# A macaron transformer trunk: cast order in the first turn, and two 512-column products behind the last transposes of x

## The chip, the cores and the metric

The kernel runs on one core of a Trainium2 chip. The metric is the device time of one launch in microseconds (us). The engines are TensorE (PE, with PEld for its weight loads), VectorE (DVE), ScalarE (ACT), GpSimd (POOL) and SyncE (SP). Each executes its own instructions in order and waits for the others through semaphores.

## The reference, cut to what matters

A sequence of 512 rows of width 1024 in float32 passes through two layers. Each has two half-step SwiGLU FFNs, one at either end, with a token mixer (differential attention in layer 0, a pooling mixer in layer 1) and a cross attention into 256 memory rows between them.

```python
D_MODEL, SEQ, DEPTH, D_FF = 1024, 512, 2, 2816

def swiglu_ffn(x, w_in, w_out):
    h = x @ w_in
    g, u = jnp.split(h, 2, axis=-1)
    return (jax.nn.silu(g) * u) @ w_out

for i in range(DEPTH):
    x = layer_norm(a * x + 0.5 * swiglu_ffn(x, ffn_w_in[i, 0], ffn_w_out[i, 0]), ...)
    ...
    x = layer_norm(a * x + h, ...)
    x = layer_norm(a * x + memory_cross_attention(x, mem, ...), ...)
    x = layer_norm(a * x + 0.5 * swiglu_ffn(x, ffn_w_in[i, 1], ffn_w_out[i, 1]), ...)
```

## The kernel before

**Pairs.** A float32 value is kept as a high part in float32r and a low part that holds the rest. A product of two such pairs is three products on PE (`mm3`, L210 to L212): high by high, the high weight by the low x (`xl`), and the low weight (`wl`) by the high x. A weight tile arrives raw by DMA. `operand` then makes its pair: a cast on ACT for the high part (`wh`, L689) and a subtraction on DVE for the low one (`wl`, L691).

**An FFN block.** There are four, starting at about 0, 750, 1080 and 1600 us; "block 1" is the first. `ffn` goes through the eleven units of 256 columns of w_in in turns of three and then two, each turn together with the w_out products of units that are finished (`down`, 512 columns wide, tiles `px`, `py`, `pz`). The first turn has units alone, in three lanes.

**A unit.** `up` computes gate and value of a unit by seven products instead of eight (Strassen-Winograd): x is cut into four parts, and products 0 to 6 are taken with those parts and with sums of them, in the order 0 (into PSUM tile x), 1 (y), 3 (z), 6 (z, added), 4 and 5 (x), 2. Each has 24 matmuls of 256 columns: two halves of 128 weight columns, four k steps, three products. The sums of x, called s1 to s4, are made on DVE by `second_factors` (L656, L661) and cut into pairs by `part` (`xe`, L125 on ACT and L126 on DVE): part 6 is s4, 4 is s2, 5 is s3. The weights of product 3 come out of those of product 0 by a DMA that adds to them in SBUF (`more`, L683, on POOL's queue, in tiles `ra`), as do the later ones; a raw tile's next add waits until its low part has been taken. Products 1 and 6 read tiles `rc`, loaded on SP's queue (L679). There are four buffers of `wh` and `wl`, four of `ra` and three of `rc`.

**Lanes.** The generators of three units are advanced in turn by `ffn`: a `yield` in `up` ends a lane's step, and the program order that results, with the scheduler's own rules and `issue_after` (an order that it must keep), sets the order on each engine. Block 1 starts while x and the weights still arrive (`at_start`). There the products of lanes 0 and 2 are taken by passes in places (`by_passes`, L716): all products on the high weights first, then those on the low ones. In this block the cast of lane 2's third operand, tile `ra`, precedes that of lane 0's `rc` for product 6.

**Blocks 2, 3 and 4** begin with the end of a layer norm: PE transposes the last rows of x (L494, eight of 128 x 128 into `pt`), between the products of the first lane, and goes on with the unit's second product, y.

Of the kernel before, what the change touches and what calls it, by code (L numbers as in the profile page):

```python
# [109 lines left out]
class Trunk:  # L110
# [407 lines left out]
    def ffn(self, layer, j, ln, beside=()):  # L518
# [58 lines left out]
        for turn in range(n):  # L577
            behind = turn == n - 1
            for step in range(1 if turn == 0 else 0, 9 if behind else 7):
                if turn == 0 and step in (2, 3):  # L580
                    next(second)
                if step == 4:
                    if behind:
                        coming = [self.plain_down(w_out, layer, j, ln, beside)]
                    else:
                        coming = start(turn + 1)
                        if at_start and turn == 0:
                            with self.tc.issue_after(self.last_load.ins):
                                next(downs[1])
                if behind and step in (4, 6, 7, 8):  # L590
                    next(coming[0])
                if behind and step > 3:
                    few(beside, 2)

                for lane, w in enumerate(works[: None if not behind or step > 1 else -1]):
                    if not (at_start and turn == 0 and lane < 2 and step == 1):
                        next(w, None)
                if turn == 1 and step == 3:
                    self.seven_of[self.waiting[0]] = self.seven(self.waiting[1])
            works = coming  # L600
# [14 lines left out]
    def second_factors(self):  # L615
# [15 lines left out]
        def part(i, x, o=slice(0, H)):  # L631
            return self.split(F[i][0][:, :, o], F[i][1][:, :, o], x)
# [21 lines left out]
        nc.vector.scalar_tensor_tensor(s2, s1, -1.0, a11, ALU.mult, ALU.subtract)  # L654
        s4 = s1
        nc.vector.scalar_tensor_tensor(s4, s2, -1.0, a12, ALU.mult, ALU.subtract)  # L656
        part(6, s4)
        yield
        part(4, s2)
        s3 = a21  # L660
# [4 lines left out]
    def up(self, w, u, lane, early, between):  # L665
# [16 lines left out]
        def more(t, *block):  # L682
            nc.gpsimd.dma_start(t, source(*block), accum_op=ALU.add)  # L683

        def operand(raw, behind=None):
            v = self.hl([P, 4, H])
            act, dve = behind or (None, None)
            with self.tc.issue_after(act.ins) if behind else nullcontext():
                hi = nc.scalar.copy(v[0], raw)  # L689
            with self.tc.issue_after(dve.ins) if behind else nullcontext():  # L690
                lo = nc.vector.tensor_sub(v[1], raw, v[0].bitcast(F32))  # L691
            splits.append((hi, lo))
            return v
# [28 lines left out]
        splits = []  # L722

        third = lane == 2
        at_start = early and self.begins is None
        sp = lambda: self.tmp("ha" if third else "sp", (P, 2, H))
        yz = "py" if third else "yz"
        ra = load("ra", 1, 1)
# [1 line left out]
            between()  # L730
        rc = load("rc", 2, 1)
        yield
        v = operand(ra, self.turned_parts if third and at_start else None)
        if early and lane == 0:
            self.first_split = splits[0]
        more(ra, 1, 2)
# [3 lines left out]
        if at_start and lane == 0:  # L740
            by_passes(x, v, 0, (0,))
            yield
        v2 = early > 1 and operand(rc, self.turned if at_start else None)
        if v2:
            self.second_split = splits[-1]
            yield
# [5 lines left out]
        nc.scalar.copy(p1, x)  # L752
        yield
        y = bank(self.aux("y", yz))
        v2 = v2 or operand(rc, self.made_parts if third and at_start else None)
        with self.behind() if at_start else nullcontext():
            product(y, v2, 1, True, lane != 1 and at_start)
        hr = self.tmp("hr", (P, 2, S))
        h1, h2 = hr[:, :, :H], hr[:, :, H:]
        nc.vector.tensor_tensor(h1, y, p1, ALU.add)  # L760
        nc.scalar.activation(h1, h1, AF.Silu)
        yield
        v = operand(ra, self.made_parts if at_start and lane == 0 else None)
        if at_start and lane == 0:
            self.made_parts = splits[-1]
            yield
        z = bank(self.aux("z", yz))
        product(z, v, 3, True)
        more(ra, 2, 2)
        rd = load("rc", 2, 2)  # L770
        p5 = sp()
        nc.scalar.copy(p5, z)
        yield
        product(z, operand(rd), 6)
        more(rd, 1, 2)
        yield
        product(x, operand(ra), 4)
# [911 lines left out]
```

## Time and profile before

| | us |
|---|---|
| median of three runs | 1927.93 (1924.76 to 1930.44) |
| profiled execution | 1927.77 |
| its span | 1926.0 |
| PE busy | 1900.1 |
| DVE busy | 1564.4 |
| ACT busy | 1022.8 |
| POOL busy | 320.6 |

The page's times are of one profiled execution. PE's instructions overlap: a matmul starts before the one ahead of it has ended, so the distance from start to start, and not the length of one, tells how fast PE goes. A row of the timeline gives the start, the length, engine, line, operation and tiles, and in brackets how long the engine stood idle before it and which engine ended that. The granted clock is the share of full speed that the chip allowed PE.

### The profile page before, as it was taken

Reading aid. Unit: us, or ns where it says so; the run is one execution under the profiler, and the core shown is the slowest. Engines: PE = TensorE matmul, PEld = TensorE weight load, DVE = VectorE, ACT = ScalarE, POOL = GpSimd, SP = SyncE. Lnnn points to the kernel's source line nnn. Section 1 sums busy time; section 2 is a strip of 40 time slices with the busy share of each in tenths; the row PEclk is TensorE's granted clock in tenths of the full one; section 3 lists DMA queues with packets and bytes.
Section 4 is the critical chain, followed back from the end, with each engine's and each line's share of the span. In section 5 each row is a group of like instructions: output and inputs, shape, how many; then the busy total and the mean of one; then the engine's idle time right before and its main releaser. Section 6 shows DMA issues by size and latency. Waiting matters only on the chain.

```text
span 1926.0 us, 32482 instructions
## 1 busy us (share of the span) xinstructions
PE 1900.1 (99%) x13066; PEld 1741.3 (90%) x13066; DVE 1564.4 (81%) x2264; ACT 1022.8 (53%) x1580; POOL 320.6 (17%) x278
## 2 busy tenths in 40 slices
PE   9999999999999999999999999999999999999998
PEld 8999998888878888999998999999899889999997
DVE  7888989888967558888888988888887568998886
ACT  6555554567755435655554655455455436555553
POOL 2112121111210002211210321112130012111210
PEclk9999999999999999999999999999999999999999
DMA  9978772322124317978686588788344437877861
GB/s 236 220 170 184 167 141 86 91 66 88 55 99 153 110 66 192 181 175 164 139 192 179 105 179 171 176 164 186 111 132 132 132 88 157 182 160 170 184 133 56
DMA packets 246742, 277.94 MB, mean 144 GB/s; under 512 B 8256, under 2 KB 212544, under 8 KB 246592
## 3 DMA queue, kind: packets, MB, share of 16 engines
q0 software_dynamic: 92928, 92.29, 31.3%
q1 hardware_dynamic: 153664, 183.59, 29.7%
q8 instruction: 102, 1.67, 0.4%
q14 instruction: 48, 0.39, 0.1%
HBM read 273.75 MB, written 2.10 MB: 143 GB/s over the span
## 4 chain that ended last, share of the span: by engine, by line
PE 77%; DVE 14%; ACT 4%; issue 2%; DMA 2%; POOL 1%; SPq 0%; DVEq 0%; ACTq 0%; POOLq 0%
PE x L210 7%; PE x L211 7%; PE x L212 7%; PE z L212 4%; PE z L210 4%; PE z L211 4%; PE ps L210 3%; PE ps L212 3%; PE ps L211 3%; PE px L210 2%; PE px L212 2%; PE px L211 2%; PE y L212 2%; DVE wl L691 2%; PE xq L210 1%
## 5 line engine op out<-in xcount | busy, mean ns | idle before, releaser
L683 POOL DMA_DIRECT2D ra<-in_ffn_w_in_dram x132 | 171.3, 1318 | 988.9 <-DVE wl L691 812.2
L689 ACT CAST wh<-ra 128x1024 fp32r<-128x1024 f32 x176 | 185.0, 1053 | 215.6 <-PE x L211 66.6
L691 DVE TENSOR_TENSOR wl<-ra,wh 128x1024 fp32r<-128x1024 f32 x176 | 214.2, 1220 | 71.2 <-ACT wh L689 70.9
L689 ACT CAST wh<-rc 128x1024 fp32r<-128x1024 f32 x132 | 138.9, 1053 | 107.6 <-PE x L211 41.8
L210 PE MATMUL x<-xe,wh 128*128 128x256 f32 x704 | 195.2, 277 | 0.0
L211 PE MATMUL x<-xe,wh 128*128 128x256 f32 x704 | 195.1, 277 | 0.0
L212 PE MATMUL x<-xe,wl 128*128 128x256 f32 x704 | 195.0, 277 | 0.0
L125 ACT CAST wh<-b 128x1024 fp32r<-128x1024 f32 x112 | 117.8, 1052 | 132.3 <-PE x L211 65.6
L691 DVE TENSOR_TENSOR wl<-rc,wh 128x1024 fp32r<-128x1024 f32 x132 | 159.7, 1219 | 27.1 <-ACT wh L689 26.1
L126 DVE TENSOR_TENSOR wl<-b,wh 128x1024 fp32r<-128x1024 f32 x112 | 136.7, 1221 | 40.8 <-ACT wh L125 40.8
L210 PE MATMUL x<-xh,wh 128*128 128x256 f32 x536 | 148.9, 278 | 0.0
L211 PE MATMUL x<-xl,wh 128*128 128x256 f32 x536 | 148.5, 277 | 0.0
L212 PE MATMUL x<-xh,wl 128*128 128x256 f32 x536 | 148.5, 277 | 0.0
L211 PEld LDWEIGHTS x<-xe,wh 128*128 128x128 f32 x704 | 132.7, 189 | 1.4
L210 PEld LDWEIGHTS x<-xe,wh 128*128 128x128 f32 x704 | 132.2, 188 | 1.3
L212 PEld LDWEIGHTS x<-xe,wl 128*128 128x128 f32 x704 | 132.2, 188 | 0.0
L126 DVE TENSOR_TENSOR wl<-raw,wh 128x1024 fp32r<-128x1024 f32 x64 | 83.0, 1301 | 42.4 <-ACT wh L125 41.6
L211 PEld LDWEIGHTS x<-xl,wh 128*128 128x128 f32 x536 | 101.0, 189 | 0.7
L210 PEld LDWEIGHTS x<-xh,wh 128*128 128x128 f32 x536 | 100.6, 188 | 0.7
L212 PEld LDWEIGHTS x<-xh,wl 128*128 128x128 f32 x536 | 100.6, 188 | 0.0
L212 PE MATMUL z<-xe,wl 128*128 128x256 f32 x352 | 98.4, 280 | 2.2 <-DVE wl L691 2.2
L211 PE MATMUL z<-xe,wh 128*128 128x256 f32 x352 | 98.3, 279 | 0.4 <-DVE xe L126 0.4
(442 smaller groups left out, 6304.0 us busy)
## 6 DMA issues: line engine op xcount, KB each, us to landing
ra<-in_ffn_w_in_dram POOLq DMA_DIRECT2D x132, 512.0 KB, 7.0
rc<-in_ffn_w_in_dram SPq DMA_DIRECT2D x88, 512.0 KB, 5.7
b<-in_ffn_w_out_dram SPq DMA_DIRECT2D x76, 512.0 KB, 4.8
ra<-in_ffn_w_in_dram SPq DMA_DIRECT2D x44, 512.0 KB, 4.8
rc<-in_ffn_w_in_dram POOLq DMA_DIRECT2D x44, 512.0 KB, 7.9
raw<-in_xa_wkv_dram SPq DMA_DIRECT2D x16, 1024.0 KB, 5.4
raw<-in_da_w_qkv_dram SPq DMA_DIRECT2D x16, 512.0 KB, 5.3
raw<-in_xa_wq_dram SPq DMA_DIRECT2D x8, 1024.0 KB, 5.1
```

Source lines behind the costliest of these rows:

```text
L125: self.nc.scalar.copy(hi, src),
L126: self.nc.vector.tensor_sub(lo, src, hi.bitcast(F32)),
L210: mm(out, w[0], x[0], start=start, stop=False, skip_group_check=again)
L211: mm(out, w[0], x[1], start=False, stop=False, skip_group_check=again)
L212: self.last_mm = mm(out, w[1], x[0], start=False, stop=stop, skip_group_check=again)
L683: nc.gpsimd.dma_start(t, source(*block), accum_op=ALU.add)
L689: hi = nc.scalar.copy(v[0], raw)
L691: lo = nc.vector.tensor_sub(v[1], raw, v[0].bitcast(F32))
```

## The change

In block 1's first turn, lane 0 makes the pair of its `rc` tile for product 6 in a step of its own, one step earlier, and lane 2's third operand is ordered behind it (`made_parts`) and behind the pair of s4 (`factor_parts`). Lane 2's product 3 is taken by passes. In blocks 2, 3 and 4 the first lane issues two products of 512 columns into y's bank, weights against weights, ahead of product 1; product 1 starts with `start=True` and overwrites them.

```diff
@@ -595,6 +595,8 @@
                 for lane, w in enumerate(works[: None if not behind or step > 1 else -1]):
                     if not (at_start and turn == 0 and lane < 2 and step == 1):
                         next(w, None)
+                    if at_start and turn == 0 and lane == 1 and step == 2:
+                        next(works[0])
                 if turn == 1 and step == 3:
                     self.seven_of[self.waiting[0]] = self.seven(self.waiting[1])
             works = coming
@@ -654,7 +656,7 @@
         nc.vector.scalar_tensor_tensor(s2, s1, -1.0, a11, ALU.mult, ALU.subtract)
         s4 = s1
         nc.vector.scalar_tensor_tensor(s4, s2, -1.0, a12, ALU.mult, ALU.subtract)
-        part(6, s4)
+        self.factor_parts = part(6, s4)
         yield
         part(4, s2)
         s3 = a21
@@ -682,12 +684,11 @@
         def more(t, *block):
             nc.gpsimd.dma_start(t, source(*block), accum_op=ALU.add)
 
-        def operand(raw, behind=None):
+        def operand(raw, *behind):
             v = self.hl([P, 4, H])
-            act, dve = behind or (None, None)
-            with self.tc.issue_after(act.ins) if behind else nullcontext():
+            with self.after([act for act, _ in behind]):
                 hi = nc.scalar.copy(v[0], raw)
-            with self.tc.issue_after(dve.ins) if behind else nullcontext():
+            with self.after([dve for _, dve in behind]):
                 lo = nc.vector.tensor_sub(v[1], raw, v[0].bitcast(F32))
             splits.append((hi, lo))
             return v
@@ -722,7 +723,7 @@
         splits = []
 
         third = lane == 2
-        at_start = early and self.begins is None
+        at_start = early > 0 and self.begins is None
         sp = lambda: self.tmp("ha" if third else "sp", (P, 2, H))
         yz = "py" if third else "yz"
         ra = load("ra", 1, 1)
@@ -730,7 +731,7 @@
             between()
         rc = load("rc", 2, 1)
         yield
-        v = operand(ra, self.turned_parts if third and at_start else None)
+        v = operand(ra, *((self.turned_parts,) if third and at_start else ()))
         if early and lane == 0:
             self.first_split = splits[0]
         more(ra, 1, 2)
@@ -740,7 +741,7 @@
         if at_start and lane == 0:
             by_passes(x, v, 0, (0,))
             yield
-        v2 = early > 1 and operand(rc, self.turned if at_start else None)
+        v2 = early > 1 and operand(rc, *((self.turned,) if at_start else ()))
         if v2:
             self.second_split = splits[-1]
             yield
@@ -752,26 +753,40 @@
         nc.scalar.copy(p1, x)
         yield
         y = bank(self.aux("y", yz))
-        v2 = v2 or operand(rc, self.made_parts if third and at_start else None)
+        v2 = v2 or operand(rc, *((self.made_parts,) if third and at_start else ()))
         with self.behind() if at_start else nullcontext():
+            if early > 1 and not at_start:
+                wide = v2[0][:, :2].rearrange("p k n -> p (k n)")
+                for _ in range(2):
+                    nc.tensor.matmul(
+                        y.rearrange("p j n -> p (j n)"), v2[0][:, 0, :P], wide, start=True, stop=True
+                    )
             product(y, v2, 1, True, lane != 1 and at_start)
         hr = self.tmp("hr", (P, 2, S))
         h1, h2 = hr[:, :, :H], hr[:, :, H:]
         nc.vector.tensor_tensor(h1, y, p1, ALU.add)
         nc.scalar.activation(h1, h1, AF.Silu)
         yield
-        v = operand(ra, self.made_parts if at_start and lane == 0 else None)
-        if at_start and lane == 0:
+        if not at_start or lane == 1:
+            v = operand(ra)
+        elif third:
+            v = operand(ra, self.made_parts, self.factor_parts)
+        else:
+            v = operand(ra, self.made_parts)
             self.made_parts = splits[-1]
             yield
         z = bank(self.aux("z", yz))
-        product(z, v, 3, True)
+        product(z, v, 3, True, third and at_start)
         more(ra, 2, 2)
         rd = load("rc", 2, 2)
         p5 = sp()
         nc.scalar.copy(p5, z)
         yield
-        product(z, operand(rd), 6)
+        v = operand(rd)
+        if at_start and lane == 0:
+            self.made_parts = splits[-1]
+            yield
+        product(z, v, 6)
         more(rd, 1, 2)
         yield
         product(x, operand(ra), 4)
```

ACT in block 1's first turn. The tiles: `ra` and `rc` are raw weights, `hr` the gate on its way through silu, `hb` and `sr` hold the sums s4, s2, s3 of x, `sp` and `ha` keep copies of the PSUM tiles x and z. Before:

```order
L752 COPY ha<-x 128x512
L689 CAST wh<-ra 128x1024
L689 CAST wh<-rc 128x1024
L761 ACTIVATE hr<-hr 128x2x256
L689 CAST wh<-rc 128x1024
L125 CAST xe<-hb 128x1024
L772 COPY sp<-z 128x512
L125 CAST xe<-sr 128x1024
L772 COPY sp<-z 128x512
L125 CAST xe<-hb 128x1024
L689 CAST wh<-rc 128x1024
L689 CAST wh<-ra 128x1024
```

Now (a line that was L689 is L690, L761 is L768, L772 is L783):

```order
L753 COPY ha<-x 128x512
L690 CAST wh<-rc 128x1024
L768 ACTIVATE hr<-hr 128x2x256
L783 COPY sp<-z 128x512
L125 CAST xe<-hb 128x1024
L690 CAST wh<-ra 128x1024
L125 CAST xe<-sr 128x1024
L783 COPY sp<-z 128x512
L690 CAST wh<-rc 128x1024
L125 CAST xe<-hb 128x1024
L690 CAST wh<-rc 128x1024
L783 COPY ha<-z 128x512
```

The first cast of `ra` stands four places further down, behind that of `rc`, a silu, a copy of z and the cast of `xe` from s4.

DVE at the same place, before:

```order
L760 TENSOR_TENSOR hr<-y,ha 128x2x256
L656 SCALAR_TENSOR_TENSOR hb<-sr,hb 128x1024
L691 TENSOR_TENSOR wl<-ra,wh 128x1024
L661 TENSOR_TENSOR hb<-hb 128x1024
L126 TENSOR_TENSOR xe<-hb,xe 128x1024
L126 TENSOR_TENSOR xe<-sr,xe 128x1024
L691 TENSOR_TENSOR wl<-rc,wh 128x1024
L126 TENSOR_TENSOR xe<-hb,xe 128x1024
L691 TENSOR_TENSOR wl<-rc,wh 128x1024 x2
L691 TENSOR_TENSOR wl<-ra,wh 128x1024 x3
```

Now (L691 is L692, L656 is L658, L661 is L663):

```order
L767 TENSOR_TENSOR hr<-y,ha 128x2x256
L658 SCALAR_TENSOR_TENSOR hb<-sr,hb 128x1024
L692 TENSOR_TENSOR wl<-rc,wh 128x1024
L663 TENSOR_TENSOR hb<-hb 128x1024
L126 TENSOR_TENSOR xe<-hb,xe 128x1024
L692 TENSOR_TENSOR wl<-ra,wh 128x1024
L126 TENSOR_TENSOR xe<-sr,xe 128x1024
L692 TENSOR_TENSOR wl<-rc,wh 128x1024
L126 TENSOR_TENSOR xe<-hb,xe 128x1024
L692 TENSOR_TENSOR wl<-rc,wh 128x1024
L692 TENSOR_TENSOR wl<-ra,wh 128x1024 x3
```

The first subtraction for `rc` moves up to where that for `ra` stood, and that for `ra` stands behind the first `xe`.

PE at the start of block 2, at the end of the transposes (X_77 is the last tile of x), before:

```order
L211 MATMUL x<-xl,wh 128x256
L212 MATMUL x<-xh,wl 128x256
L494 MATMUL pt<-ident,X_77 128x128 x8
L210 MATMUL y<-xh,wh 128x256
L211 MATMUL y<-xl,wh 128x256
L212 MATMUL y<-xh,wl 128x256
```

Now:

```order
L211 MATMUL x<-xl,wh 128x256
L212 MATMUL x<-xh,wl 128x256
L494 MATMUL pt<-ident,X_77 128x128 x8
L761 MATMUL y<-wh 128x512 x2
L210 MATMUL y<-xh,wh 128x256
L211 MATMUL y<-xl,wh 128x256
L212 MATMUL y<-xh,wl 128x256
```

Two products of 512 columns stand between the transposes and y. Blocks 3 and 4 have the same two rows at the same place. In blocks 2 and 3 the scheduler also moves some casts of `ra` and `rc` on ACT and their subtractions on DVE ahead of those for `xe`; on POOL one add to an `rc` tile moves ahead of one to an `ra` tile in block 1; SP's order stays.

## The prediction

> **What bounds the kernel now.** I read the page first: the busy times, then the chain that ended last.
>
> ```profile
> span 1926.0 us, 32482 instructions
> PE 1900.1 (99%) x13066; PEld 1741.3 (90%) x13066; DVE 1564.4 (81%) x2264; ACT 1022.8 (53%) x1580; POOL 320.6 (17%) x278
> PE 77%; DVE 14%; ACT 4%; issue 2%; DMA 2%; POOL 1%; SPq 0%; DVEq 0%; ACTq 0%; POOLq 0%
> ```
>
> PE is busy for 1900.1 of 1926.0 us, so there are two ways to gain: fill its few gaps, or make its products follow each other faster. So I looked at windows of 10 us, where PE's count matters more than its busy share.
>
> ```profile
> 30.00:40.00 10.00, 8.48 (x70) 7.87 (x68) 7.06 (x8) 7.22 (x10) 2.56 (x2) 1.00 1.20 216
> 40.00:50.00 10.00, 8.93 (x64) 8.93 (x65) 7.57 (x7) 4.53 (x6) 6.47 (x5) 0.83 0.88 126
> 60.00:70.00 10.00, 10.00 (x91) 10.00 (x90) 9.01 (x11) 4.81 (x7) 0.00 (x0) 1.00 1.10 337
> 780.00:790.00 10.00, 10.00 (x87) 10.00 (x87) 5.93 (x5) 3.46 (x4) 5.99 (x5) 1.00 1.18 179
> 1610.00:1620.00 10.00, 9.27 (x77) 8.68 (x76) 10.00 (x11) 7.49 (x10) 3.88 (x3) 1.00 0.50 98
> ```
>
> The columns are the window, its length, busy us and count of PE, PEld, DVE, ACT and POOL, the granted clock, the DMA share and GB/s. Two things stand out. In the first block's first turn (30 to 50 us) PE has gaps, and the granted clock falls to 0.83. And at 780 us, in block 2, a PE that is just as full at clock 1.00 starts 87 products in 10 us where block 1 starts 91.
>
> **The gap in block 1.** PE's timeline there:
>
> ```profile
> 34.85 0.28 PE L211 MATMUL z<-xl,wh 128*128 128x256 f32 x1
> 35.15 0.38 PE L212 MATMUL z<-xh,wl 128*128 128x256 f32 x1
> 37.75 0.36 PE L210 MATMUL z<-xe,wh 128*128 128x256 f32 x1
> 38.51 0.38 PE L211 MATMUL z<-xe,wh 128*128 128x256 f32 x1 [0.40 <-DVE xe L126]
> 41.07 0.53 PE L212 MATMUL z<-xe,wl 128*128 128x256 f32 x1 [2.17 <-DVE wl L691]
> 44.39 0.36 PE L212 MATMUL z<-xe,wl 128*128 128x256 f32 x1
> 50.72 0.28 PE L210 MATMUL x<-xe,wh 128*128 128x256 f32 x1
> 44.94:80.64 35.70, 35.70 (x317) 35.70 (x316) 26.49 (x34) 19.18 (x25) 7.91 (x7) 1.00 1.16 259
> ```
>
> The last row, a window, gives the full pace: some 315 products in 35.70 us, 0.1133 us from start to start. The three lanes' product 6 (3 x 24 = 72 products) takes 50.72 - 37.75 = 12.97 us instead of 72 x 0.1133 = 8.16: 4.81 us lost. Some 3.2 us of it is two waits, for product 6's left operand (`xe`, DVE) and for the low part of lane 0's weights (`wl`). The rest follows from them: from 41.07 to 44.39 there are 15 steps from product to product, 0.22 us each, nearly double, and the granted clock of that window is 0.83. A small wait at 35.15 adds about 0.3 (0.30 instead of 0.11 to its start, and 0.1 behind it). Together 5.1 us.
>
> Why `xe` and `wl` are late stands on ACT and DVE, and in two transfers:
>
> ```profile
> 27.80 0.57 ACT L752 COPY ha<-x 128x512 f32<-128x512 f32 x1
> 32.78 1.05 ACT L689 CAST wh<-ra 128x1024 fp32r<-128x1024 f32 x1 [4.41 <-DMA ra<-in_ffn_w_in_dram]
> 33.74 1.05 ACT L689 CAST wh<-rc 128x1024 fp32r<-128x1024 f32 x1
> 36.16 1.04 ACT L125 CAST xe<-hb 128x1024 fp32r<-128x1024 f32 x1
> 30.31 0.69 DVE L760 TENSOR_TENSOR hr<-y,ha 128x512 f32<-128x512 f32 x1
> 30.91 1.22 DVE L656 SCALAR_TENSOR_TENSOR hb<-sr,hb 128x1024 f32<-128x1024 f32 x1
> 33.87 1.23 DVE L691 TENSOR_TENSOR wl<-ra,wh 128x1024 fp32r<-128x1024 f32 x1 [1.74 <-ACT wh L689]
> 39.80 1.22 DVE L691 TENSOR_TENSOR wl<-rc,wh 128x1024 fp32r<-128x1024 f32 x1
> 13.90 5.50 SPq L679 DMA_DIRECT2D rc<-in_ffn_w_in_dram  x2
> rc<-in_ffn_w_in_dram SPq DMA_DIRECT2D x1, 512.0 KB, 13.1
> ```
>
> ACT executes in order and stands 4.41 us at the cast of lane 2's third operand (call it ra2'), whose data an accumulating DMA brings at 32.7. Behind it wait the cast of lane 0's `rc` (rd0), a silu, and the cast of `xe`. Yet rd0 had been issued at 13.90 and took 13.1 us (the last row, for that issue), so it was there at 27.0.
>
> **What the change makes of it.** It puts rd0's cast ahead of ra2', and the silu, the copy of z and the cast of `xe` as well. Working through with the durations above (on ACT one starts about 0.95 after the one before, on DVE 1.14):
> - ACT: rd0 at 28.3, within the former wait; the silu at 31.05, since DVE's `hr` ends at 31.0; the copy of z at about 32.1, when lane 1 takes over from lane 0 on PE; `xe` at 32.6 (s4, the DVE row at 30.91, ends at 32.13); ra2' at 33.5 to 34.6.
> - PE asks for ra2' where it does now, one product ahead of 34.85, at 34.74: no wait, or at most 0.25 us if a step of ACT slips.
> - DVE: rd0's low part at 32.05, the next sum at 33.2, `xe`'s low part at 34.3 to 35.5, ra2's low part at 35.45 to 36.7. PE now takes lane 2's z in passes: 16 products on the high part, then one of product 6, then 8 on the low part, which begins at 34.74 + 17 x 0.113 = 36.7: just in time again.
> - Then product 6 has both operands from 37.6 on; the low parts of lanes 1 and 2 (37.75 and 40.05 on DVE) are done 1 to 2 us ahead of PE.
>
> So PE runs through and product 6 ends at about 45.7 instead of 50.72: **-5.0 us**. From both sides: 5.1 if nothing is late, and 4.6 if both "just in time" places each slip a quarter of a microsecond. No operation is added in block 1. What lies behind must come 5 us earlier too: weights. The tightest of the later casts waits for a DMA even now:
>
> ```profile
> 71.38 1.05 ACT L689 CAST wh<-ra 128x1024 fp32r<-128x1024 f32 x1 [3.15 <-DMA ra<-in_ffn_w_in_dram]
> 72.46 1.23 DVE L691 TENSOR_TENSOR wl<-ra,wh 128x1024 fp32r<-128x1024 f32 x1 [2.50 <-ACT wh L689]
> 77.92 0.28 PE L210 MATMUL x<-xh,wh 128*128 128x256 f32 x1
> ```
>
> Its low part is done at 73.7, and its product starts at 77.92 and needs the low part two products later, at 78.15. Of these 4.4 us of cover nothing is left if that transfer stays where it is: 0.6 us lost, and 1 to 2 us if a second cast is late in the same way. But it should move too, because buffers come free earlier and the DMA engines have room in 40 to 50 us (share 0.88), so I take nothing off.
>
> The rule that I weigh here is in the Trainium skill, "TensorE: Matmul & The Clock Gate", section "What's actually happening": the array drops to half rate after an idle window of some 3.4 us and needs about as long of work to come back. The trace agrees: 3.2 us of waits, then 3.3 us at nearly doubled pitch. By it a rest of wait of half a microsecond costs only itself.
>
> **The two products in blocks 2, 3 and 4.** Here PE doesn't wait; it is in a slower rhythm. The same 256-column product comes in two paces:
>
> ```profile
> 761.80:818.22 56.42, 56.42 (x482) 56.42 (x480) 48.36 (x57) 35.13 (x46) 14.19 (x11) 1.00 0.88 169
> 1088.60:1145.01 56.41, 56.41 (x481) 56.41 (x480) 48.13 (x57) 33.94 (x45) 14.22 (x11) 1.00 0.92 180
> 1616.82:1659.80 42.98, 42.98 (x381) 42.98 (x381) 35.73 (x44) 24.70 (x32) 12.95 (x10) 1.00 1.10 209
> 821.02:826.48 5.46, 5.46 (x50) 5.46 (x48) 5.46 (x6) 2.74 (x3) 1.27 (x1) 1.00 0.45 128
> 1078.44:1081.37 2.93, 2.93 (x26) 2.92 (x25) 2.93 (x5) 0.84 (x1) 2.60 (x2) 1.00 1.05 158
> 760.81 1.03 PE L494 MATMUL pt<-ident,X 128*128 128x128 f32 x8
> 761.60 0.36 PE L210 MATMUL y<-xh,wh 128*128 128x256 f32 x1
> 818.22 0.40 PE L210 MATMUL px<-wh,ha 128*128 128x512 f32 x1
> 743.41 1.04 PE L494 MATMUL pt<-ident,X 128*128 128x128 f32 x8
> 744.20 0.48 PE L210 MATMUL ps<-q,oT 128*128 128x512 f32 x1
> 744.75 0.40 PE L212 MATMUL ps<-q,oT 128*128 128x512 f32 x1
> ```
>
> A window's count takes in a product or two at its ends. In blocks 2 and 3 some 479 products follow the transposes at 56.42 / 479 = 0.1178 us, without a wait; block 4, which has waits in its z, comes out of them at 42.98 / 380 = 0.1131. A pace, once taken, holds until something of another width or a wait comes. Behind 512-column products the 256-column ones are fast: the row 821.02:826.48 is 48 of them (0.1138), and so are all such places of the turns that follow. The exception is the row 1078.44: 24 products in 2.93 less the transposes' start, at 0.1178, behind 18 products of 512. So a product of 512 columns gives the fast pace mostly, not always.
>
> Cost: the rows from 743.41 show transposes followed by 512 columns: the first starts 0.79 behind the transposes, as y does now (760.81, 761.60), and the third product starts 744.75 - 744.20 = 0.55 later. So y's first product comes 0.55 later, while its second follows at 0.12 instead of 0.20 (761.60 and the window's start at 761.80): **+0.47 us** net for a block. Gain, if y falls into the fast pace: 480 x (0.1178 - 0.1133) = 2.15 us, so **-1.68 us** for block 2 and the same for block 3. The ends are +0.47 and -1.68 a block; I take the fast one, by the many 512-column runs that end so.
>
> The scheduler also moves casts forward in blocks 2 and 3 (ra and rc ahead of `xe`). They land more than 2 us before PE asks, also at the fast pace, so they count for nothing; DVE is 5.93 busy of 10 in 780 to 790, which leaves room to catch up. In block 4 the 0.47 us go into waits that are there today: PE stands at 9.27 in 1610 to 1620 while DVE is busy for 10.00 of 10.00, and DVE's chain, not PE's start, sets when PE goes on. So **0**; without that cover +0.47, and +1.7 if the waits now end in the slow pace (380 x 0.0045).
>
> A page speaks against this part: the Trainium skill, "TensorE: Matmul & The Clock Gate", section "Wait — 56ns, not 53.3ns?", gives a warm product of N columns one fixed distance, N / 2.4 GHz plus 2.5 ns, an estimate of 109 ns for 256 and 216 for 512. By that there is no second pace, and six more products only cost 6 x 0.216 = 1.3 us. The windows above measure 113 and 118 for the same shape, so the measurement decides that two paces exist; whether two products switch them, no row shows.
>
> **The sum.** Against the profiled execution's 1927.77 us (1926.0 of span and 1.8 around it; the median of the runs is 1927.93): -5.0 - 2 x 1.68 + 0 = -8.4, so **1919.5 us**.
>
> **Rivals.**
> 1. *The pace stays slow behind the two products.* For it: the row at 1078.44, and that the slow pace also follows the transposes directly. Against it: the row at 821.02. Then 1927.8 - 5.0 + 2 x 0.47 = 1923.7 us. The page's rule above gives nearly the same time.
> 2. *Part of block 1's gain is lost*: a transfer sets the later casts (1 to 2 us, above), or the "just in time" place at 34.6 leaves a small wait behind which the slow pace holds, some 400 products x 0.0045 = 1.8 us; or block 4 falls into the slow pace (+1.7). With fast blocks 2 and 3: about 1921.4. Against it: PE's gaps at 35.15 and 38.51 both ended in the fast pace.
> 3. *Slower: the slow pace holds beyond the first turn.* The turns behind it alternate 48 products of 256 columns with 12 of 512, 8.2 us together. At 0.1178 the 48 take 5.65 instead of 5.46; 12 of 512 in the slow pace take 821.02 - 818.22 = 2.80 where the fast take 8.2 - 5.46 = 2.74: +0.25 for a pair, and some 26 pairs from 821 to 1035 make +6.5 us a block. With blocks 2 and 3 so: 1927.8 - 5.0 + 0.9 + 13 = 1936.7. It decides from 16 pairs on. Against it: today the slow first turn runs into 818.22 and comes out fast at 821.02.
> 4. *The cast order doesn't come about on the chip as in the program* (ra2' needed earlier than I work out, and PE's wait only moves): block 1 then gains 0 to 2, and with fast blocks 2 and 3 the total is 1922.4 to 1924.4. For it: two places are just in time. Against it: the wait of 4.41 us, with rd0's data there.
>
> **How the numbers follow.** Forecast 0.54; rival 1 0.20; rival 2 0.10; rival 3 0.10; rival 4 0.06. A measurement here tells no change from a change of 0.3%, or 5.8 us: faster is below 1922.1. That holds for the forecast and half of rival 2: 0.59. Same: rivals 1 and 4 and the rest of 2: 0.31. Slower: rival 3, 0.10. Range: from 1916.5, where block 1 gives 5.1, block 4 turns out fast too and the turn behind starts a bit earlier, to 1925.5, which takes in rivals 1 and 2 and part of 4.
>
> **What would show it.** Right: in 30 to 50 us PE starts some 88 in each 10 us at clock 1.00, ACT has no wait of 4 us, and x's first product behind product 6 starts near 45.7; in 780 to 790 PE starts 91, and px of block 2 starts about 1.7 us earlier relative to y's transposes. Wrong: ACT still waits at `wh<-ra` with `xe` behind it; 87 in 780 to 790; or under 48 products in 5.5 us behind 821.

## The result, and the profile after

The changed kernel takes **1921.58 us** (median of seven runs, 1920.15 to 1922.73) against 1927.43 for the kernel before (seven runs). The ratio is 0.9972, with a 95% interval of 0.9961 to 0.9982: 5.9 us or 0.3% less, just at the bound of what a measurement tells from no change, where the prediction said 1919.5 and 8.4 us. The profiled execution took 1921.52 us, its span 1919.7, so 6.3 us less than the profiled execution of before (1926.0 of span). This is the windows view of the changed kernel (window, length, busy us and count of PE, PEld, DVE, ACT and POOL, granted clock, DMA share, GB/s):

```profile
30.00:40.00 10.00, 10.00 (x88) 9.94 (x88) 10.00 (x10) 8.13 (x11) 4.27 (x4) 1.00 1.20 218
40.00:50.00 10.00, 10.00 (x88) 10.00 (x86) 6.27 (x6) 4.47 (x5) 6.04 (x5) 1.00 1.24 199
60.00:70.00 10.00, 10.00 (x87) 10.00 (x86) 6.60 (x8) 4.49 (x5) 1.28 (x1) 1.00 1.07 371
780.00:790.00 10.00, 10.00 (x91) 10.00 (x90) 5.53 (x6) 4.26 (x5) 3.37 (x3) 1.00 1.22 192
1100.00:1110.00 10.00, 10.00 (x91) 10.00 (x90) 6.79 (x6) 5.30 (x6) 6.75 (x6) 1.00 1.05 162
```

The gap in block 1 is gone: 88 products in each of the first two windows, where 70 and 64 stood, and the clock is 1.00. At 780 and 1100 us PE starts 91 instead of 87; for 1100, this was the row of the kernel before:

```profile
1100.00:1110.00 10.00, 10.00 (x87) 10.00 (x86) 9.36 (x9) 6.88 (x9) 6.09 (x5) 1.00 1.07 156
```

But the row 60:70, which had 91, now has 87: block 1 has taken on the slow pace that blocks 2 and 3 lost. The starts of the same instructions in the two PE timelines show where the time went:

| start of | before | changed | difference | gained since the row above |
|---|---|---|---|---|
| first px, block 1 | 80.64 | 77.56 | -3.08 | -3.08 |
| last transposes of x, block 2 | 760.81 | 758.04 | -2.77 | +0.31 |
| first px, block 2 | 818.22 | 813.78 | -4.44 | -1.67 |
| last transposes of x, block 3 | 1087.60 | 1083.11 | -4.49 | -0.05 |
| first px, block 3 | 1145.01 | 1138.85 | -6.16 | -1.67 |
| last transposes of x, block 4 | 1602.84 | 1596.38 | -6.46 | -0.30 |
| first px, block 4 | 1659.78 | 1653.38 | -6.40 | +0.06 |

Three of the four terms came out as predicted in this pair of profiles: -1.67 for blocks 2 and 3 each (-1.68 was said) and +0.06 for block 4 (0). Block 1 gave 3.08 instead of 5.0. Its timeline, ACT's row first, then DVE's, then PE's:

```profile
33.94 1.04 ACT L690 CAST wh<-ra 128x1024 fp32r<-128x1024 f32 x1
34.65 1.22 DVE L126 TENSOR_TENSOR xe<-hb,xe 128x1024 fp32r<-128x1024 f32 x1
35.79 1.22 DVE L692 TENSOR_TENSOR wl<-ra,wh 128x1024 fp32r<-128x1024 f32 x1
35.04 0.38 PE L717 MATMUL z<-xh,wh 128*128 128x256 f32 x1
37.07 1.19 PE L717 MATMUL z<-xh,wl 128*128 128x256 f32 x8
77.56 0.40 PE L210 MATMUL px<-wh,ha 128*128 128x512 f32 x1
38.10:77.56 39.46, 39.46 (x338) 39.46 (x336) 31.21 (x40) 22.38 (x29) 9.51 (x8) 1.00 1.15 254
```

Lane 2's third operand, once the cause of a wait of 4.41 us, is cast at 33.94 and wanted at 35.04. Its low part is ready at 35.79 + 1.22 = 37.01, and the low pass begins at 37.07. That is the "just in time" place: the pass of eight takes 1.19 us where seven steps of 0.113 and one length of 0.28 make 1.07. The 0.1 us is nothing. What follows is not: from 38.10 to px 335 products take 39.46 us, 0.1178 each.

Behind the transposes of block 2:

```profile
758.04 1.03 PE L494 MATMUL pt<-ident,X 128*128 128x128 f32 x8
758.83 0.71 PE L761 MATMUL y<-wh 128*128 128x512 f32 x2
759.38 0.28 PE L210 MATMUL y<-xh,wh 128*128 128x256 f32 x1
813.78 0.39 PE L210 MATMUL px<-wh,ha 128*128 128x512 f32 x1
759.38:813.78 54.40, 54.40 (x482) 54.40 (x480) 47.29 (x57) 34.85 (x45) 14.17 (x11) 1.00 0.92 175
1084.45:1138.85 54.40, 54.40 (x481) 54.40 (x480) 47.34 (x57) 33.52 (x44) 14.19 (x11) 1.00 0.94 184
```

The two products take 0.55 us (759.38 - 758.83), as worked out, and the 480 behind them take 54.40 us, 0.1133 each, where the kernel before needed 56.42 for 479.

### The profile page after: what moved, and what is told of

Its sections match the earlier page's. It is cut to its first block, busy times and chain, and to the rows that moved or that the text cites. A ratio compares the mean times of both kernels' runs of the same rounds, so it can differ in the third digit from the quotient of the medians.

```text
span 1919.7 us, 32489 instructions
## 1 busy us (share of the span) xinstructions
PE 1895.9 (99%) x13072; PEld 1738.2 (91%) x13072; DVE 1563.6 (81%) x2264; ACT 1023.4 (53%) x1580; POOL 319.8 (17%) x278
## 4 chain that ended last, share of the span: by engine, by line
PE 78%; DVE 13%; ACT 4%; DMA 2%; issue 2%; POOL 1%; SPq 0%; DVEq 0%; ACTq 0%; POOLq 0%
PE x L210 7%; PE x L211 7%; PE x L212 7%; PE z L212 4%; PE z L210 4%; PE z L211 4%; PE ps L210 4%; PE ps L212 4%; PE ps L211 4%; PE px L210 2%; PE px L212 2%; PE px L211 2%; PE y L212 2%; PE xq L210 1%; PE xq L211 1%
## 5 line engine op out<-in xcount | busy, mean ns | idle before, releaser
L690 ACT CAST wh<-ra 128x1024 fp32r<-128x1024 f32 x176 | 185.1, 1054 | 207.5 <-PE x L211 66.5
L692 DVE TENSOR_TENSOR wl<-ra,wh 128x1024 fp32r<-128x1024 f32 x176 | 213.9, 1220 | 67.1 <-ACT wh L690 66.4
L690 ACT CAST wh<-rc 128x1024 fp32r<-128x1024 f32 x132 | 138.9, 1053 | 104.9 <-PE x L211 40.4
L125 ACT CAST wh<-b 128x1024 fp32r<-128x1024 f32 x112 | 117.8, 1052 | 128.9 <-PE x L211 65.1
L692 DVE TENSOR_TENSOR wl<-rc,wh 128x1024 fp32r<-128x1024 f32 x132 | 159.8, 1218 | 26.8 <-ACT wh L690 26.8
L125 ACT CAST wh<-raw 128x1024 fp32r<-128x1024 f32 x64 | 66.5, 1049 | 59.3 <-PE xq L211 21.0
```

The lines of the kernel that those rows point to most:

```text
L125: self.nc.scalar.copy(hi, src),
```

## The experiments

In what follows the "distance" of a block is that from the start of the last single transpose (0.03 us ahead of what follows it) to the first px: 56.65 us in blocks 2 and 3 before, 54.98 in the changed kernel. Each profile is one execution; the times are medians, and each ratio is to runs of the kernel before on the same chip.

**1. The first turn alone.**

```diff
-            if early > 1 and not at_start:
...
-                for _ in range(2):
-                    nc.tensor.matmul(..., v2[0][:, 0, :P], wide, start=True, stop=True)
```

> The changed kernel without its six products of 512 columns: only the first turn's order. Theory A (the two products set the pace of blocks 2 and 3, the cast order sets block 1, and nothing else matters): block 1's first px starts at 77.6 as in the changed kernel, 3.1 us earlier than before; in blocks 2 and 3 the distance from the last transposes to px is 57.4 us again, at 87 products in 10 us; time 1927.4 - 3.0 = 1924.4. Theory B (blocks 2 and 3 got faster because everything ahead of them moved, so that the pace fell otherwise): the distance stays near 55.8 and the time near 1921.5.

Measured: 1922.34 us, ratio 0.9976 (0.9965 to 0.9987). The profiled execution (1920.18, the fastest of its seven runs) was faster than A allowed, and its windows and rows say why:

```profile
38.10:75.72 37.62, 37.62 (x335) 37.62 (x333) 29.58 (x36) 20.86 (x27) 9.18 (x8) 1.00 1.17 261
756.49:810.78 54.29, 54.29 (x482) 54.29 (x480) 47.04 (x57) 35.03 (x46) 14.22 (x11) 1.00 0.92 175
1081.14:1137.56 56.42, 56.42 (x482) 56.42 (x481) 48.16 (x57) 33.95 (x45) 14.22 (x11) 1.00 0.92 181
```

Block 1 ends in the fast pace here (px at 75.72, 4.9 us earlier than in the first profile of before), with the same cast order. Block 2 is fast without any 512-column product (54.29 for some 480), and block 3 slow (56.42). So neither A nor B as put: against that profile the cast order does give the full 4.9 us where the pace stays fast, and block 2's pace isn't the same in every execution. What differs in block 2 lies ahead of the transposes: the first product's run x is slow there (0.1178), where it was fast (0.1133) in the profile of before.

**2. The six products alone**, on the kernel before.

```diff
         with self.behind() if at_start else nullcontext():
+            if early > 1 and not at_start:
...
+                for _ in range(2):
+                    nc.tensor.matmul(..., v2[0][:, 0, :P], wide, start=True, stop=True)
             product(y, v2, 1, True, lane != 1 and at_start)
```

> The kernel before with the six products of 512 columns alone. Theory A: px of block 1 at 80.6 as before, blocks 2 and 3 55.8 us from the last transposes to px, 1.66 less each, block 4 unchanged within 0.2; time 1927.4 - 3.3 = 1924.1. Theory B: blocks 2 and 3 at 57.4 or more, +0.47 each, time 1928.4.

Measured: 1925.84 us, ratio 0.9991 (0.9983 to 1.0), less than A said, and its interval reaches no change at all; the profiled execution (1926.58) was the slowest of the eleven.

```profile
762.72:817.17 54.45, 54.45 (x481) 54.42 (x480) 47.39 (x57) 34.85 (x45) 14.16 (x11) 1.00 0.91 175
1087.82:1142.25 54.43, 54.43 (x481) 54.40 (x480) 47.38 (x57) 33.56 (x44) 14.19 (x11) 1.00 0.95 185
1612.20:1658.46 46.26, 46.26 (x396) 46.26 (x394) 37.75 (x46) 26.20 (x34) 13.38 (x11) 1.00 1.03 194
1610.72 0.38 PE L212 MATMUL z<-xh,wl 128*128 128x256 f32 x1 [0.87 <-DVE wl L691]
```

Blocks 2 and 3 are fast, as A has it. Only block 3 tells for the products, though: x of block 2 is slow here, and in number 1 y came out fast behind a slow x without them. Block 4 was slow behind its wait for DVE: some 393 products in 46.26 us, 0.1177 each, and its distance grew from 56.17 to 57.87. That took back 1.7 us in this execution. The casts' 0.24% and the products' 0.09% add up to the change's 0.28% within their intervals.

A misses in block 1: px starts at 79.15 and not at 80.6, with the old cast order and the same wait of 2.17 us for `wl` ahead of 41.02. The clock tells why. In all fourteen traces the granted clock switches only at whole multiples of 3.413 us from the first switch. These are such stretches around the wait, the first two in the profile of before, the last two here:

```profile
37.74:41.15 3.41, 0.83 (x5) 0.44 (x3) 3.21 (x4) 3.41 (x5) 0.00 (x0) 1.00 1.04 159
41.15:44.57 3.42, 3.42 (x16) 3.42 (x17) 3.42 (x4) 1.27 (x2) 2.04 (x2) 0.50 0.33 33
35.94:39.35 3.41, 2.66 (x22) 2.27 (x20) 2.21 (x3) 3.41 (x6) 0.67 (x1) 1.00 1.23 194
39.35:42.77 3.42, 1.75 (x15) 1.75 (x16) 3.42 (x4) 3.02 (x4) 1.28 (x1) 1.00 0.57 91
```

Before, the wait filled one stretch nearly whole (PE busy for 0.83 us), and the next one ran at 0.50. Here it is split between two stretches (2.66 and 1.75 us busy), and the clock stays at 1.00. Number 8 has the dip again, behind a stretch with 1.58 us. The mean clock of a whole run shows it too: 0.998 in both profiles with the dip, 0.999 here. Of the 66 timed runs of the kernel before beside the experiments, 36 have 0.998 or less, and their medians are 0.6 to 1.6 us above those of the other 30 on each of the four occasions; of number 2's eleven, five have 0.998. All runs with the new cast order have 0.999.

**3. No wait at the low pass.** DVE's sum s3 behind lane 2's low part:

```diff
+            self.third_parts = splits[-1]
...
-        nc.vector.tensor_tensor(s3, a11, a21, ALU.subtract)
+        with nullcontext() if self.begins else self.tc.issue_after(self.third_parts[1].ins):
+            nc.vector.tensor_tensor(s3, a11, a21, ALU.subtract)
```

> The changed kernel, with DVE's sum s3 ordered behind the low part of lane 2's third operand, which is then ready some 0.8 us before PE asks for it. Theory A (the 0.09 us that PE waits for this low part at 37.28 puts all that follows into the slow pace, 342 products at 0.1178): the wait is gone, the products from 35 us to px stay at 0.1133, px starts at 77.6 - 1.6 = 76.0, time 1921.6 - 1.6 = 1920.0. Theory C (the slow pace there has another cause, such as the denser load of casts and transfers): 87 or 88 products in 10 us remain, px at 77.4 to 77.6, time 1921.5.

Measured: 1920.48 us, ratio 0.9965 (0.9952 to 0.9977). In this execution weights arrived about 1 us later at the start of the block, so that px starts at 77.24; the pace is what answers.

```profile
36.49 1.22 DVE L693 TENSOR_TENSOR wl<-ra,wh 128x1024 fp32r<-128x1024 f32 x1
38.26 1.07 PE L718 MATMUL z<-xh,wl 128*128 128x256 f32 x8
38.50:77.24 38.74, 38.74 (x344) 38.74 (x343) 30.92 (x37) 21.76 (x29) 9.82 (x8) 1.00 1.17 259
```

The low part is ready at 37.71, half a microsecond ahead of the pass; the pass takes 1.07 us, and some 342 products behind it take 38.74 us, 0.1133 each. C is out: the same casts and transfers with the same density run at the fast pace when the wait is gone. That the wait is what decides isn't shown by this one execution, since number 9 stays fast with it.

**4. Two 512-column products in block 1**, behind lane 2's z.

```diff
+        if third and at_start:
+            idle = self.aux("idle", "py")
...
+                for _ in range(2):
+                    self.last_mm = nc.tensor.matmul(idle, v[0][:, 0, :P], wide, start=True, stop=True)
```

> The changed kernel with two more products of 512 columns in block 1, into a bank that nobody reads, right behind the low pass of lane 2's z (38.1 us). Theory A (a 512-column product ahead of a run of 256 ones puts it into the fast pace, wherever it stands): the slow pace from 37.28 lasts for 8 products only, the 334 behind it go at 0.1133; -334 x 0.0045 + 0.46 = -1.0 us, px at 76.5, time 1920.5. Theory C: the pace behind them stays 0.1178, px at 78.0, time 1922.0.

Measured: 1920.23 us, ratio 0.9965 (0.9952 to 0.9979), its five runs within 0.8 us. Behind the products the run to px is fast, as A has it:

```profile
38.93:76.91 37.98, 37.98 (x337) 37.98 (x335) 29.83 (x36) 21.08 (x27) 9.06 (x8) 1.00 1.17 260
```

But the wait at the low pass had left the fast pace already in this execution, so the row doesn't show that the products turned it.

**5. One product instead of two** in blocks 2 to 4 (`range(1)` for `range(2)`).

> The changed kernel with one 512-column product instead of two behind the last transposes of x. The scheduler then leaves the casts of blocks 2 and 3 in their old order. Theory A (the pace is set by the last distance from start to start ahead of the run; 203 or 204 ns behind the transposes is followed by the slow pace, 205 and more by the fast one): one product leaves a distance of some 315 ns, so y is fast in blocks 2 and 3, 0.23 us shorter than with two: 54.75 us from the last transpose to px, time 1921.3. Theory D (it takes two, because only 230 to 236 ns between 512-column products is followed by the fast pace; or the new cast order of blocks 2 and 3 is what helps): y is slow, 56.65 + 0.3, time 1925.

Measured: 1920.79 us, ratio 0.997 (0.9958 to 0.9982), and block 2 in the profile:

```profile
757.81 0.48 PE L761 MATMUL y<-wh 128*128 128x512 f32 x1
758.12 0.28 PE L210 MATMUL y<-xh,wh 128*128 128x256 f32 x1
758.12:812.54 54.42, 54.42 (x482) 54.41 (x480) 47.55 (x57) 34.95 (x46) 14.22 (x11) 1.00 0.92 175
```

One is enough: fast in both blocks, behind a fast x, with a distance of 54.75. The cast order of blocks 2 and 3 is nearly the old one here (on ACT one cast of an `rc` and one of an `xe` stand exchanged), and number 6 has the same order and a slow block 2, so D falls in both its parts.

**6. Two products of 256 columns instead of 512.**

```diff
-                        y.rearrange("p j n -> p (j n)"), v2[0][:, 0, :P], wide, start=True, stop=True
+                        y[:, 0], v2[0][:, 0, :P], wide[:, : 2 * P], start=True, stop=True
```

> The changed kernel with two products of 256 columns in place of the two of 512. Theory A (width makes the last distance; 256 columns behind transposes stay at 203 to 205 ns): the run falls as it would without them, slow where x ahead of it was fast: block 3 at 56.65 + 0.24 = 56.9 us from the last transpose to px, and 87 products in 10 us; time some 2 to 4 us above the changed kernel's. Theory E (any delay of two more products switches the pace): fast, 54.75, time 1921.

Measured: 1922.23 us (1921.29 to 1926.03), ratio 0.9981 (0.9972 to 0.999).

```profile
759.60:816.21 56.61, 56.61 (x483) 56.61 (x482) 47.89 (x57) 35.08 (x46) 14.19 (x11) 1.00 0.88 168
1086.70:1141.16 54.46, 54.46 (x483) 54.46 (x482) 47.55 (x57) 33.82 (x45) 14.25 (x11) 1.00 0.95 187
```

Block 2 is slow (481 products at 0.1177), block 3 fast (0.1132). In both the distance behind the transposes is 202 ns; x ahead of them was slow in block 2 and fast in block 3, and y has the pace of x. So A, which had block 3 slow, misses, and E, which had both fast, falls in block 2: the delay isn't what helps, and two narrow products leave the pace open where a wide one leaves the fast pace.

**7. Lane 2's product 3 without passes** (`product(z, v, 3, True)` in block 1).

> The changed kernel with lane 2's product 3 in block 1 taken as before (three products for each tile) instead of by passes. The low part, ready at 37.0 in the changed kernel, is then wanted by the third product at 35.3. Theory A: a wait of 1.7 us there, so px at 76.0 + 1.7 = 77.7 with the fast pace behind the wait; the cast order without the passes gives some 3 us of the 4.7. Theory F (the passes don't matter, the low part is made earlier once it is wanted earlier): no wait over 0.3 us, px at 76.0 to 77.6.

Measured: 1920.75 us, ratio 0.9967 (0.9955 to 0.9979), so no loss against the changed kernel.

```profile
35.18 0.28 PE L211 MATMUL z<-xl,wh 128*128 128x256 f32 x1
35.30 0.28 PE L210 MATMUL z<-xe,wh 128*128 128x256 f32 x1
35.87 0.39 PE L211 MATMUL z<-xe,wh 128*128 128x256 f32 x1 [0.29 <-DVE xe L126]
36.09:78.02 41.93, 41.93 (x357) 41.93 (x357) 33.82 (x42) 24.28 (x31) 10.31 (x8) 1.00 1.14 248
```

The expected wait of 1.7 us isn't there: after two products of lane 2's z the scheduler goes on with lane 0's product 6 and leaves lane 2's low products for later. PE waits 0.57 - 0.11 us for `xe`, and the run behind that wait is slow (0.1178), px at 78.02. Both theories miss: the low part isn't made earlier, as F had it, but wanted later, and px is 0.4 us behind F's range by the slow pace. The times show no worth of the passes; the cast order carries the gain.

**8. The kernel before, profiled again.**

> The kernel before, profiled once more, to see which of the paces come back. Theory A (transposes flip the pace: behind a fast x they leave a slow y and the other way round): in block 3, where x is fast in each profile so far, y is slow again, 56.65 us; in block 2 y is slow if x was fast and fast if x was slow; in block 4 x is slow and y fast. Theory G (each run falls by chance): block 3 is fast about every second time.

Measured, one execution: 1929.55 us.

```profile
44.05:81.74 37.69, 37.69 (x323) 37.69 (x321) 29.09 (x38) 19.65 (x25) 8.65 (x7) 1.00 1.12 250
761.70:818.14 56.44, 56.44 (x482) 56.44 (x481) 48.38 (x57) 35.16 (x46) 14.19 (x11) 1.00 0.89 169
1088.50:1144.94 56.44, 56.44 (x481) 56.44 (x480) 48.17 (x57) 33.98 (x45) 14.22 (x11) 1.00 0.92 181
1613.73:1661.46 47.73, 47.72 (x402) 47.52 (x403) 39.47 (x47) 27.67 (x36) 14.26 (x11) 1.00 1.00 188
```

Blocks 2 and 3 are slow again behind a fast x, as A has it; for G block 3 would have had to be fast about every second time. Blocks 1 and 4, fast behind their waits in the first profile, are slow this time, so A's fast y of block 4 did not come: PE waits behind y's third product, and what follows is slow. px of block 1 starts 1.1 us later, and block 4 is 1.7 us longer. By their pace these two places alone put 2.8 us between two executions of one kernel, whose times differ by 1.8.

**9. The changed kernel once more.**

> The changed kernel once more. Theory A (pace behind a small wait is a matter of some ns, so block 1 can fall either way; behind 512-column products it is fast): blocks 2 and 3 are 54.98 us from the last transpose to px again; block 1's px lies at 76.0 to 76.5 if the wait at the low pass leaves the fast pace, at 77.6 if the slow one; time 1920 to 1922.7. Theory C (the denser load makes block 1 slow): px at 77.4 to 77.7 with 87 products in 10 us again.

Measured: 1921.36 us (1919.15 to 1923.27), ratio 0.9971 (0.9961 to 0.9981). Blocks 2 and 3 as before; block 1 fell the other way:

```profile
37.61:76.39 38.78, 38.78 (x343) 38.78 (x343) 30.96 (x37) 22.34 (x29) 10.32 (x8) 1.00 1.17 258
```

Some 342 products at 0.1134, px at 76.39, so C is out again.

**10. A version from what was learned**: number 3, one product instead of two in blocks 2 to 4, and one ahead of lane 2's z in block 1.

```diff
+        if third and at_start:
...
+            nc.tensor.matmul(z.rearrange("p j n -> p (j n)"), v[0][:, 0, :P], wide, start=True, stop=True)
         product(z, v, 3, True, third and at_start)
```

> The changed kernel with s3 behind lane 2's low part, one 512-column product instead of two in blocks 2 to 4, and one ahead of lane 2's product 3 in block 1 (into the bank that this product then overwrites). Theory A: no wait behind that product, so block 1 runs at 0.1133 from 35 us to px in every execution, blocks 2 and 3 take 54.75; time 1921.6 - 2 x 0.23 + 0.23 - 1.5 where the changed kernel is slow in block 1, so 1919.5 to 1920 and a narrow spread. Theory C: block 1 at 87 products in 10 us, time 1921.

Measured: **1919.89 us** (1918.87 to 1920.52), ratio 0.9962 (0.9949 to 0.9976), the lowest of all, though its interval overlaps with that of the changed kernel.

```profile
34.91:75.70 40.79, 40.79 (x361) 40.79 (x360) 33.13 (x39) 23.99 (x31) 10.31 (x8) 1.00 1.18 255
```

360 products at 0.1133, px at 75.71: block 1 gives 4.9 us against the first profile of before.

**11. The same with one such product ahead of lane 2's z in the other blocks** (`third and early`).

> As the one before, with the 512-column product ahead of lane 2's product 3 in blocks 2, 3 and 4 too. Theory A: block 4 is then fast behind its waits in every execution (it was slow in three of ten profiles, at 57.87 instead of 56.2), which is worth 0.3 x 1.5 us on the mean; blocks 2 and 3 pay 0.23 each for nothing: the time is 0 to 0.5 us above best1's, its spread a little narrower. Rival: the product itself waits for its bank or puts a run into the slow pace: 2 us more.

Measured: 1924.25 us, ratio 0.9986 (0.9978 to 0.9995): 4.4 us worse than number 10. The rival was right:

```profile
770.56 0.39 PE L783 MATMUL z<-wh 128*128 128x512 f32 x1
770.79 0.28 PE L210 MATMUL z<-xh,wh 128*128 128x256 f32 x1
757.00:770.50 13.50, 13.50 (x121) 13.50 (x120) 13.50 (x16) 11.29 (x15) 3.66 (x3) 1.00 0.53 101
770.79:813.20 42.41, 42.41 (x362) 42.40 (x361) 33.98 (x42) 23.58 (x30) 10.30 (x8) 1.00 0.99 191
```

Ahead of it 120 products in 13.5 us; behind it 360 in 42.41, 0.1178. A single 512-column product in a stretch of products at 0.1133, without a wait, turned the pace to 0.1178, in blocks 2 and 3 both. Block 4 was fast (56.20), as A has it.

**12. Two there instead of one.**

> As the last kernel (best2), but with two 512-column products instead of one ahead of lane 2's product 3 in blocks 2, 3 and 4 (block 1 keeps one). Theory H (in a fast run without a wait one such product turns the pace to slow, and a second one turns it back, as two did in block 1): blocks 2 and 3 go on fast behind them, 54.75 + 2 x 0.23 = 55.2 us from the last transpose to px, time 1921. Theory I (at this place any 512-column product leaves the slow pace, for instance by the distance of 232 ns): 56.6 + 0.23 = 56.8 and time 1924.5.

Measured: 1923.05 us (1920.91 to 1924.21), ratio 0.9982 (0.9973 to 0.9991). In the profiled execution, the fastest of eleven, H holds:

```profile
771.81:812.62 40.81, 40.81 (x361) 40.81 (x360) 33.44 (x42) 23.60 (x30) 10.31 (x8) 1.00 1.03 198
```

360 products at 0.1134 in block 2, and the same in block 3. But the median is 2 us above that execution, so others must have lost time where this one didn't; no profile shows where.

## Why the prediction was right, and where not

**Block 1, the order.** Right. ACT's wait of 4.41 us had the cast of lane 0's `rc` and of `xe` behind it; with those ahead of it PE has no gap and the granted clock no dip. Where the pace stays fast this is worth 4.9 us against the first profile (numbers 1 and 10), next to the -5.0 of the sum, and in number 1 x's first product behind product 6 starts at 45.80, where 45.7 was said. The casts that waited for transfers later didn't limit it. But the sum took the clock's dip for a part of every execution. It put 15 steps of 0.22 us on it, 1.6 us more than at 0.1133. In number 2, without the dip, px of the old order comes 1.5 us earlier than in the first profile, so there the new order is worth some 3 us (79.15 against 75.72, with a start of lane 2's y that is 0.56 us later). That the forecast was made from an execution with the dip, and that its 5.0 met 4.9, is partly luck.

**Block 1, the size.** This is the term that was mis-sized: -5.0 said, -3.08 measured in the profile. The step that failed is "PE runs through". The prediction called two places just in time and priced a slip at 0.25 us; the slip at 37.07 was 0.1 us, and the run behind it cost 335 x 0.0045 = 1.5 us more: PE's steps are 0.113 up to the slip and 0.118 from the second product of the low pass on. That price stood in the second rival (some 400 products, 1.8 us), whose time of about 1921.4 us is nearer to the measured one than the forecast. So it does not hold that a rest of wait costs only itself. Number 3 takes the wait away and the pace stays fast, but a slip doesn't always turn it. How often it does is less clear: it did in one of the two profiles of the changed kernel, and in none of four others that have a slip at this place (numbers 1, 4, 5 and 6). Another 0.26 us is the block's start, where y of lane 2 began at 26.73 instead of 26.47.

**The time before.** The sum was made against an execution of 1927.77 us. In further runs beside the experiments the kernel before had medians of 1925.9 to 1926.7. The first profile was thus 1.1 to 1.9 us above the middle, and part of what the forecast has too much is that; about half of those runs show no dip of the clock (number 2).

**Blocks 2 and 3.** Right in place and size in the first pair of profiles (-1.67 each). The 0.55 us for the two products and the 0.0045 us for a product both held, and the rule that the prediction set aside (the Trainium skill, "TensorE: Matmul & The Clock Gate", section "Wait — 56ns, not 53.3ns?", one fixed distance for a product of N columns) does not hold here, with 0.1133 and 0.1178 us for the same product: by it the two products could only have cost time. What was incomplete is the picture of "a pace, once taken, holds": the prediction counted the slow pace as given in the kernel before. Number 1 shows block 2 fast without any added product, behind a slow x. Where that happens, there is nothing to gain and 0.47 us to lose, and x of block 2 was slow in six of the fourteen profiles; that it was fast in both profiles of the first pair, and block 2's term met in full, is luck. Block 3 has no such doubt: x is fast in all fourteen profiles, y behind it is slow in the three without an added product and fast in all ten with 512-column ones. So it is no surprise that the medians show less than the profile: the products alone gave 0.09%, about 1.7 us of 3.3 (0.8 us by the two medians), and an interval that reaches zero.

**Block 4.** Right: +0.06 where 0 was said. The risk that was named, the slow pace behind its wait, came in numbers 2, 6 and 8, each time with a distance of 57.87 us; that it stayed away in the first pair is luck.

**The slower side.** It did not come: the turns behind px ran as before in each profile. That a 512-column product can also turn the pace from 0.1133 to 0.1178, which number 11 shows, was not among the rivals.

**Small slips of the working.** By their rows the two waits ahead of 41.07 are 3.1 us (0.65 and 2.45) and not 3.2, the sum from 1927.77 is 1919.4, and rival 3 needs some 20 pairs (10 us at 0.5 us for a pair in both blocks) and not 16 to be 0.3% slower. None of them moves the forecast. Nor does a pace always hold until a wait or another width comes: near 1446.7 us of the changed kernel's profile a run of 256-column products goes from 0.118 to 0.113 over steps of 0.121 and 0.116.

## What to carry to other kernels

Where PE is busy throughout, count its products in equal windows: a few per cent between stages with the same shapes and the same granted clock may be a gain that no busy share shows. And a wait of a tenth of a microsecond in a long run of equal products may cost fifteen times its length behind it, so an operand that is "just in time" should be made early by as much as the order allows. Where an execution can fall either way, one profile isn't enough; take the pieces from profiles and the sum from many timed runs.

## What the runs showed of the hardware

Products of 256 columns in fp32r follow each other at 113.3 or 117.8 ns at a granted clock of 1.00, for hundreds of products on end. The pace goes with what leads into such a stretch. This counts it over all fourteen profiles, for stretches of at least twenty, from the starts of PE's instructions, by the pace of their first twenty. The distance is the step from the 512-column product to the first of the stretch, or, behind eight or sixteen transposes, the step from its first product to its second. The kernel's last stage, with steps of 120 to 125 ns among the others, is left out.

```
ahead of the stretch          distance, ns    then 113    then 118
transposes                    200 to 202             4          52
transposes                    203 to 204             0          42
transposes                    205 to 208            37           0
512 columns                   225 to 227             0          40
512 columns                   230 to 236          1472           2
512 columns                   314 to 341            15           0
```

Behind transposes the distance tells the pace from 203 ns on, as theory A of number 5 had it, and a nanosecond or two divides the cases. It often, but not always, means that the pace swaps: 39 of the 42 in the second row had products at 113 ahead of the transposes, and 25 of the 37 in the third had 118. That fits number 1: there x ahead of the transposes of block 2 was slow, and y came out fast. The distance may be no more than a first sign of the pace that follows. One 512-column product within a stretch at 113 ns turned it to 118 (number 11: the two exceptions in the fifth row), two did not (numbers 4 and 12), and one behind transposes left 113 (number 5). It looks like a phase that some instructions shift; which one, and why, no run settles.

The granted clock fell to 0.50 for one stretch of 3.413 us behind a stretch in which PE was busy for 0.83 or 1.58 us, and did not behind 1.75 or 2.66 us. So the same wait of PE costs a dip of the clock or none, by where it lies between the clock's possible switches (number 2).
